# One decoder layer in fp32 on one core: the steps up to the first gate and up products in another order of the table

## The chip, the cores and the metric

The kernel runs on 1 core of one Trainium2 chip. The time is device microseconds (us) of one execution; below, the median of the runs. A core has engines that run side by side, each with its own program that it works through in order: TensorE (PE in the profile, with PEld for its weight loads), VectorE (DVE), ScalarE (ACT), GpSimd (POOL), and SyncE (SP), which here issues nearly all DMAs. An engine waits at an instruction until what it needs has been signalled by the others.

## The reference, cut to what matters

One layer over 512 tokens of width 1024, all in float32: a token mixer between two norms, then a SwiGLU channel mixer between two norms.

```python
h = rms_norm(x, attn_pre_norm)
proj = h @ w_in                       # q, k, v of both head groups, gates
# group A: differential attention, 4 heads, two 64-wide maps each, 128-wide values
p = softmax(mask(q @ k.T * scale)); a = p[0] - lam * p[1]; o = rms_norm(a @ v, diff_subln) * 0.2
# group B: 8 query heads, 2 key/value groups, three branches with sigmoid gates
kc, vc = (silu(blocks(t) @ w1) @ w2 for t in (kc_tok, vc_tok))
o = gate0 * attend(q, kc, vc) + gate1 * attend_selected(q, ks, vs) + gate2 * attend_window(q, kw, vw)
x = x + rms_norm(concat(o_A, o_B) @ w_out, attn_post_norm)
h = rms_norm(x, ffn_pre_norm)
f = (silu(h @ w_gate) * (h @ w_up)) @ w_down
x = x + rms_norm(f, ffn_post_norm)
```

## The kernel before

**Products.** A float32 product is made of three faster ones: each operand is split into a high and a low half (ACT writes the high half, DVE or POOL subtracts it from the operand), and PE multiplies high by high, low by high and high by low into one PSUM tile. So weights come by DMA (`wraw`), are split (`whi`, `wlo`), and are used; activations likewise (`xh`, `xl`; `pth`, `ptl` for attention weights; `oh`, `ol` for head outputs).

**Stages.** The opening loads x and the first weights. Then come the projections (`fm`, `v`, `g` tiles) with the rotary embedding of their results, which go to DRAM (`qk`) and are read back with heads apart (`qst`, `kst`); beside them the compressed keys and values (`cx`, `cst`, `cmp`). Then for each of 12 heads scores (`sc`), maxima, exponentials, scaling, transposes (`tr`), splits of these and the products with the values (`av`); for the compressed branch `scc`, `pc`. The heads' outputs meet the output projection (`mixp`, `mix`), two norms (steps on `u`, `x`, `mixt` with row factors `rr`, transposes `trh`) give the input of the channel mixer, and its first gate and up products (`gu`) follow. These stages overlap. After them come, in loops that the change does not touch, the rest of the gate and up products (`gw`, `block_mul`, L1250) and the down products (`acc`, L1461).

**Order.** The part up to the first gate and up products is written as 32 streams. Each is a Python generator that emits the instructions of one kind of step and yields between steps. A table in the source, `TABLE` (L51), says letter by letter which stream makes its next step; the driver is three lines (L1163 on):

```python
need = {t: next(g) for t, g in streams.items()}
for t in TABLE:
    need[t] = next(streams[t], "end")
```

All instructions of the streams go through a wrapper, `Written` (L222), which keeps them on each engine in the order in which they were emitted. So the table alone fixes, for PE, DVE, ACT, POOL and for SP's queue of DMAs, which instruction stands behind which. (Through the wrapper, all of them have line L230 in the profile; they are told apart by their tiles.) Waits between engines and the rotation of buffers follow from that order: a tile tag has a fixed number of buffers (PSUM: mm 2, tr 2, av 1 and three score tags of 1), and a step that takes a buffer waits for the last reader of the one before it.

The letters that the prediction names, with their function: a `x_loads` L255, b `x_highs` L280, d `constants` L321, S `weights` L419 (a weight's load on SP, its high half on ACT, its low half on DVE), P `projections` L434 (a step is four matmuls of a projection's 24, or some of a compression or value product), R `evictions` L499 (rotary steps on DVE and the store to `qk`), K `compression` L575, Q `loads` L723 (`qst`, `kst`), A `scores` L744, X `maxima` L759, Y `scalings` L788 (on POOL, ACT or DVE by row block), Z `transposes` L814, L `lows` L835 (`ptl`), V `values` L844, O `outputs` L868, J `heads` L894 (the differential heads' norm and the split of all outputs), W `out_weights` L941 (the output projection's weights, and those of the first two gate and up blocks F0 and F1), M `mixes_` L983 (three matmuls each), w, x, y, z `norms` L1129 for the four token blocks, F `gates_` L1140. A step is named by its letter and its number within the letter, from 0: R40 is the 41st R of the table.

Of the kernel before, what the change touches and what calls it, by code (L numbers as in the profile page):

```python
# [48 lines left out]
HEADS = "D2 D3 N4 N5 N6 N7 D0 D1 N0 N1 N2 N3"  # L49
WORDER = "2 3 6 7 0 1 F0 4 5 F1"  # L50
TABLE = (  # L51
    "aaabbcaabbaaPcbPbcbaPaPbaaPbabcPPPPaaccPcPbPbPPPbPPbPcbPPcPdPbdcdPbPPcPbcPSPbcPcPPPPcPPPPcedPPPSSSSeePeP"
    "ePPPPaaPdSeeeRePPeRRSSRRRPRPPPSRPRSRPRSPPPSRRPKPRPPPPRSRPPRPSPSSSaKKPPPPPPPRRSPPPPPSSPSRRRRSSPPPPPRRdRKK"
    "KSRRSKSdPKPKRRRPSPQSdSPSPSSPRSPSPPKSRKKKKKdSRPPSPKKRPdSRdKKPPSRRRSSSdSPPPKdRKKKKKKKPPQSPRRSSKRPSPPPSSPAA"
    "SXPSQEXRRPSRPASPPQRKKPRPPSPSSXXARSARQXPPSEAPXRPKPQKESXGSPRPEESPKSKRPRAdAXPRSSKXdXEKESPRGRRRRPAPPEXGPRRPE"
    "RYRPPPPPRYYYXGPRRPPRGRYPYEYYYPPGSGSPSPPQRPQGGGEZQZQPHPLASAQERXXZAEQHXXARGGSSSSRPEEPERXSYPPGEAXXEGPAPAGYA"
    "HLGXVPRYAELXVREPEXYPSAGEVPVXEOXOYPGXSREPAPERRYRYRPSJJXJYSTPTYZSRRYXTJRPATAPHXZPSLYREJEZPQPAYPRESRJHPSHLX"
    "SRRRRRPJXPAEYYVYPLXZZRPREAPWRXXHRRYJEHVLXPPEEYAZRVHVSRXPWOPQAPOYYPYYWLRSZLHPYWSVLAEYXZXHLZAXWXVPAVRHYXPL"
    "VZYARHYXLEPPPRWVZVHZLPEPTAHESXTRAPVEPEEYVEXWAQVZHYPLWERZPXWPLROHWLWAYEJOWJZWJVPPJYQHXWVYYXLPVXRRAXTVVWYQ"
    "QRWYYVVEEEVTVRZAOHZAEAOJXHLRXLZYEJYHRMZJQARJHEELVMYVVYQRLXVEXYZHYXMRXZAALEEYYQVVHXVZLMAQHLVUZVZYXEJHXYJX"  # L60
    "AHELXALMEZOAAZUHXYHOXXLLYAMYGYVYVZGEVYYYHVGVYGMXLEEUWWEGVXZHZGVGEVLQVHGMOZMQEGHOGMEALLJEJXXAGAVXGEQUEYEY"
    "AQXMGXEGAYVXXEGGWVVMOMEAMGUOWYWGATXAXTJTMYYYYXEMTAJJYEZXJUHZAHWYMMXEALJEWWXLZMYYYYYYYYQXMEZEAJEXHLVWVHZJ"
    "MAXHALEEWVEVLZXWOYYMZOHQAYYXXELHEXAVYVLWXYYYJJEVZEVAAHXJEJEZLVXVHXVZLAJVEEVZMXOAHMXOHLEYLYWJWZZAJXAVHHLE"
    "ELXXYVTTZVYHYYJVXVZAWYLXVAWYWWMMEYHEEZLMHZEHXMLVVTEJYTWLVYOMWZZHYMOLVVJYYYHYZJWVVHLYLVZHMWLVYYZZVVVHHLML"
    "OZOHZLHMVVLZWWWVZHVLHLVVWVVVWOWOMOJOMMJJMMMMJBBBBNBNNNBwwwwwNxNxxwxxwxxxwwwxwwWNwNNNNxWNxwNxxwxwwNxwwxxx"
    "xxwwwNxNxxNxNWWWWNNNyWWyNyNNzyyzFFyyzFyzyFFzzzzyyyFFyzyzyFzyWzzzzyWFyyzzyyFzzzyyyzFzzFz"
)
HP = 400
POOL_LO = "157"
# [1631 lines left out]
```

## Time and profile before

| | |
|---|---|
| median of 3 runs | 654.77 us (654.54, 654.77, 657.61) |
| the profiled execution | 658.55 us |
| its span, first to last instruction | 656.5 us |
| mean granted TensorE clock in it | 0.991 |
| instructions in the span | 11115 |
| busy: PE, DVE, ACT, POOL | 636.7, 545.3, 390.6, 94.4 us |
| chain that ended last, by engine | PE 77%, DVE 12%, DMA 4%, ACT 3% |

The profile is that of one execution, the profiled one, which took some microseconds longer than the median. An engine's busy time counts its instructions from start to end; matmuls are pipelined, so a busy PE is not always one at its peak. In a timeline line the first number is the start in us from the span's start, the second how long the instruction or group took; the bracket at its end gives the idle time before it and what ended that. The chain that ended last is followed back from the last instruction through whatever released each step.

### The profile page before, as it was taken

What the parts mean: (1) busy time and instruction counts of PE and PEld (TensorE: products, weight loads), DVE (VectorE), ACT (ScalarE), POOL (GpSimd) and SP (SyncE); (2) the same over time, 40 slices, a digit from 0 to 9 for tenths busy, and PEclk for the clock granted to TensorE, in tenths of its full rate; (3) what the DMA queues carried; (4) which work ended last, traced back from release to release, by engine and by line L of the source; (5) the groups of instructions that cost most, each with busy time, mean ns of one, the idle gap of its engine ahead of it and who ended that gap; (6) DMA issues with size and microseconds to landing.
All of it is one profiled execution on the core that took longest, in us unless ns stands there. A gap on an engine that the chain in (4) does not pass through costs nothing.

```text
span 656.5 us, 11115 instructions
## 1 busy us (share of the span) xinstructions
PE 636.7 (97%) x4081; PEld 569.9 (87%) x4081; DVE 545.3 (83%) x1050; ACT 390.6 (59%) x821; POOL 94.4 (14%) x100
## 2 busy tenths in 40 slices
PE   9899899999999999999999999999999999999995
PEld 5788789788988888887898999999999998888884
DVE  5757887789789798978999998888888639999866
ACT  7334554575567688955756655655655539675434
POOL 0000001112316236532200000000000101120023
PEclk9799999999999899999999999999999999999999
DMA  8354796715315423145414333223223547984543
GB/s 307 124 162 185 251 309 231 237 36 202 136 35 206 137 106 113 65 178 205 163 34 142 115 103 123 97 97 129 97 97 129 127 131 203 307 257 132 199 90 128
DMA packets 32902, 100.52 MB, mean 153 GB/s; under 512 B 4176, under 2 KB 5072, under 8 KB 31952
## 3 DMA queue, kind: packets, MB, share of 16 engines
q1 hardware_dynamic: 30544, 95.62, 41.8%
q0 software_dynamic: 2304, 4.20, 3.8%
q8 instruction: 32, 0.52, 0.3%
q14 instruction: 22, 0.18, 0.1%
HBM read 85.64 MB, written 12.06 MB: 149 GB/s over the span
## 4 chain that ended last, share of the span: by engine, by line
PE 77%; DVE 12%; DMA 4%; ACT 3%; issue 2%; SPq 0%; DVEq 0%; ACTq 0%
PE gw L1250 28%; PE acc L1461 17%; PE fm L230 9%; PE av L230 4%; PE v L230 4%; PE sc L230 3%; PE mix L230 3%; PE tr L230 3%; PE g L230 2%; DMA wraw<-in_wf 2%; PE scc L230 1%; DVE rr L230 1%; DMA qk<-rope 1%; DVE mixt L230 1%; PE mixp L230 1%
## 5 line engine op out<-in xcount | busy, mean ns | idle before, releaser
L230 POOL TENSOR_TENSOR p<-p,l 128x384 f32<-128x384 f32 (+3 forms) x60 | 54.5, 939 | 126.0 <-DVE l L230 101.3
L230 ACT ACTIVATE p<-p,nm 128x128 f32<-128x128 f32 (+1 forms) x96 | 53.2, 556 | 12.3 <-DVE nm L230 10.3
L230 DVE CUSTOM_DVE_ANT_0 p<-sc,mask_b 128x128 f32<-128x128 f32 (+1 forms) x96 | 44.6, 483 | 7.1 <-PE sc L230 5.5
L230 ACT ACTIVATE whi<-wraw 128x1024 fp32r<-128x1024 f32 (+2 forms) x34 | 34.9, 1034 | 24.3 <-issue 13.1
L230 DVE TENSOR_TENSOR wlo<-wraw,whi 128x1024 fp32r<-128x1024 f32 (+2 forms) x34 | 40.9, 1209 | 8.6 <-ACT whi L230 8.6
L230 ACT ACTIVATE pth<-tr 128x384 fp32r<-128x384 f32 (+1 forms) x60 | 30.7, 521 | 25.1 <-PE tr L230 22.6
L230 DVE TENSOR_TENSOR ptl<-tr,pth 128x384 fp32r<-128x384 f32 (+1 forms) x60 | 35.2, 595 | 10.4 <-ACT pth L230 10.2
L230 PE MATMUL sc<-kst,qst 128*128 128x128 f32 (+1 forms) x192 | 41.3, 331 | 2.2 <-DMA kst<-qk 1.5
L1396 POOL DMA_DIRECT2D dr<-in_wd x8 | 7.0, 880 | 235.8 <-DVE wu L1284 189.3
L230 PE MATMUL fm<-xh,whi 128*128 128x512 f32 x128 | 35.4, 403 | 0.5 <-ACT whi L230 0.5
L230 PE MATMUL fm<-xh,wlo 128*128 128x512 f32 x128 | 35.0, 401 | 0.0
L230 PE MATMUL fm<-xl,whi 128*128 128x512 f32 x128 | 33.7, 394 | 0.0
L230 PEld LDWEIGHTS sc<-kst,qst 128*128 128x128 f32 x192 | 28.8, 189 | 5.3 <-DVE vn L230 1.9
L230 PE MATMUL tr<-ident,p 128*128 128x128 f32 x200 | 31.4, 280 | 1.4 <-DVE ptl L230 1.3
L230 PE MATMUL mix<-ws,oh 128*128 128x512 f32 x84 | 29.6, 403 | 0.0
L230 PEld LDWEIGHTS tr<-ident,p 128*128 128x128 f32 x200 | 24.2, 144 | 5.6 <-DVE ptl L230 1.8
L230 PEld LDWEIGHTS fm<-xl,whi 128*128 128x128 f32 x128 | 24.2, 190 | 5.0
L230 PEld LDWEIGHTS fm<-xh,wlo 128*128 128x128 f32 x128 | 24.1, 192 | 4.9
L230 PEld LDWEIGHTS fm<-xh,whi 128*128 128x128 f32 x128 | 23.5, 192 | 5.0 <-ACT whi L230 1.0
L1461 PE MATMUL acc<-whi,ah 128*128 128x512 f32 x60 | 23.5, 392 | 0.0
L1461 PE MATMUL acc<-whi,al 128*128 128x512 f32 x60 | 23.5, 392 | 0.0
L1461 PE MATMUL acc<-wlo,ah 128*128 128x512 f32 x60 | 23.5, 392 | 0.0
(368 smaller groups left out, 1956.0 us busy)
## 6 DMA issues: line engine op xcount, KB each, us to landing
wraw<-in_wg SPq DMA_DIRECT2D x22, 512.0 KB, 3.3
dr<-in_wd SPq DMA_DIRECT2D x22, 512.0 KB, 4.5
wu<-in_wu SPq DMA_DIRECT2D x19, 512.0 KB, 3.2
wraw<-in_wf SPq DMA_DIRECT2D x16, 512.0 KB, 4.7
qk<-rope SPq DMA_DIRECT2D x7, 1024.0 KB, 4.9
qst<-qk SPq DMA_DIRECT2D x24, 256.0 KB, 2.7
kst<-qk SPq DMA_DIRECT2D x24, 256.0 KB, 4.1
wraw<-in_wo SPq DMA_DIRECT2D x8, 512.0 KB, 3.3
```

Of the source, the lines that this page charges most:

```text
L230: r = getattr(self.eng, name)(*a, **k)
L1250: m = pe.matmul(pt, ww[:, k * P:(k + 1) * P], hx[k], start=(start and n == 0), stop=(n == 11), skip_group_check=True)
L1396: pool.dma_start(t[:, H], wd[pair(p)[0]][:, L], accum_op=OP.add)
L1461: m = pe.matmul(pt, x, y, start=(start and n == 0), stop=(stop and n == 2), skip_group_check=True)
```

## The change

The 1543 letters of `TABLE` are put in another order. Each letter occurs as often as before, so each stream makes the same steps in the same order within itself, and the instructions are the same. Between the streams the order differs: on PE some 1320 of 1787 instructions of this part stand in the same order to one another in both kernels, on DVE 327 of 517, on ACT 237 of 373, on POOL 70 of 76, in SP's queue 107 of 126; none moves by more than about 56 places on PE. The rest of the source, the other tables of order, the buffer counts and the choice of engines are unchanged.

The first and the last three lines of the table in the diff (the eleven between them change in the same manner):

```diff
 TABLE = (
-    "aaabbcaabbaaPcbPbcbaPaPbaaPbabcPPPPaaccPcPbPbPPPbPPbPcbPPcPdPbdcdPbPPcPbcPSPbcPcPPPPcPPPPcedPPPSSSSeePeP"
...
-    "ELXXYVTTZVYHYYJVXVZAWYLXVAWYWWMMEYHEEZLMHZEHXMLVVTEJYTWLVYOMWZZHYMOLVVJYYYHYZJWVVHLYLVZHMWLVYYZZVVVHHLML"
-    "OZOHZLHMVVLZWWWVZHVLHLVVWVVVWOWOMOJOMMJJMMMMJBBBBNBNNNBwwwwwNxNxxwxxwxxxwwwxwwWNwNNNNxWNxwNxxwxwwNxwwxxx"
-    "xxwwwNxNxxNxNWWWWNNNyWWyNyNNzyyzFFyyzFyzyFFzzzzyyyFFyzyzyFzyWzzzzyWFyyzzyyFzzzyyyzFzzFz"
+    "aaaabbbcPcPaPPcaabbPaPaPcbPPPbacPPacPbPPPaPPPPbbPPbcPSPPPbPcbaPPPPPPPPabbcdbbaPSSdabcccbPScccceePPPPSSeP"
...
+    "LYJXAYZYMTEJYXHZELVJXVZVEVVHVVJXAWLEZVVYMYWHEMXHOLETLZYMYYOTHZVYYYYYYVLZHVVVHLJLZHMYZVVLZVWHHVOLYLZMZWJO"
+    "HMHVLLVZZWWWWVHHVLVVLWVVVMOOOOMMMWJJJWJWMBBBBMMBMMNMBWWWwwNwwNNNwNxwwxxxxxxwxNNNwwxwwNxwWxwNxxxxwNwNwwNx"
+    "xxxxNNWNNwWwwxwxxxNNNNNyyyzyWyyzNyyFFzzzyzFFzFFyWFzWyyzFyyFzyyzzzyzyyyzFzzzzzFyFyyzyzzz"
 )
```

More of the change, by code (lines that the diff above doesn't have):

```diff
@@ L51 @@
 TABLE = (
-    "aaabbcaabbaaPcbPbcbaPaPbaaPbabcPPPPaaccPcPbPbPPPbPPbPcbPPcPdPbdcdPbPPcPbcPSPbcPcPPPPcPPPPcedPPPSSSSeePeP"
[L53 to L61, printed above, removed]
@@ L62 @@
-    "AQXMGXEGAYVXXEGGWVVMOMEAMGUOWYWGATXAXTJTMYYYYXEMTAJJYEZXJUHZAHWYMMXEALJEWWXLZMYYYYYYYYQXMEZEAJEXHLVWVHZJ"
-    "MAXHALEEWVEVLZXWOYYMZOHQAYYXXELHEXAVYVLWXYYYJJEVZEVAAHXJEJEZLVXVHXVZLAJVEEVZMXOAHMXOHLEYLYWJWZZAJXAVHHLE"
-    "ELXXYVTTZVYHYYJVXVZAWYLXVAWYWWMMEYHEEZLMHZEHXMLVVTEJYTWLVYOMWZZHYMOLVVJYYYHYZJWVVHLYLVZHMWLVYYZZVVVHHLML"
-    "OZOHZLHMVVLZWWWVZHVLHLVVWVVVWOWOMOJOMMJJMMMMJBBBBNBNNNBwwwwwNxNxxwxxwxxxwwwxwwWNwNNNNxWNxwNxxwxwwNxwwxxx"
-    "xxwwwNxNxxNxNWWWWNNNyWWyNyNNzyyzFFyyzFyzyFFzzzzyyyFFyzyzyFzyWzzzzyWFyyzzyyFzzzyyyzFzzFz"
+    "aaaabbbcPcPaPPcaabbPaPaPcbPPPbacPPacPbPPPaPPPPbbPPbcPSPPPbPcbaPPPPPPPPabbcdbbaPSSdabcccbPScccceePPPPSSeP"
@@ new lines @@
+    "eeePPPPPPeeRSeeRRRaSRPPRPPPPPRRPRRRKPPSSPRdRddSPPPSRRPSPPSPRPPSSPRKPPRPRKPPPKSSSPdPPSSPRRPKRPSSSPRPKKRdR"
+    "RRRRKSPSSKRPPPPSPQRPSSSSPPPPPPdSSKSKKSPRPKPKdKSKRKSKPRKPSSSPPPdRRPSRRSPPPRRRSKKKKSKdKKRSRQPSPKSSKSQdPPSP"
+    "PPPSSSASAXEAXPQRPRKSSPPPKPRdKKPQPXARSRASdPXRXAQRSGSXEXREKPPARXPXPEKSEEASEEKdPASRSRPRPXKPPPPRRYRPGGPYRRRP"
+    "RPRRXPPGEPYYRRRPPPPEPPGYPGGYGRRYSYRSYZGQGQZQPHPSQGPESPXHRRLRPRSPAAAXSPPQXPSPESESRZXGHEXAVSPRXEEGPGYYAXPL"
+    "LXEVSPSAAPXPPYGYARRXYXEXGVVRPAEQOAROYASEJGEPRPXPERYYGPEEXTRXJJYSXRAZSRAHESPEPPSJLTZPEJYXHXSTRRRYPYRXEYAT"
@@ new lines @@
+    "ZPEAJYQLPPRREHJPZLARXVHXLVZPVYSPZRRWRRYHRYXXYAELRPXHEVAZOOYAYREPLPPZHVEVYXVRAAVHYPRLYYZEELPVPYTSQHXJTSPV"
+    "EXXWPWLZZHXRPWWEAPQEPHRXASLVXLVVPYZPYOEXYPAHRLOEZQEAEHAXXYWZPPLPHXZWWPWWWWEERRPLYPYYJWHLVYVVVVRTRARVVXVW"
+    "JRVRTZAJYAERJXRZOHOAJLYXEXYWHEZMQLQHJALRZQJEJZVHQEYYYYXHLXVVXMJMRZYAMHYEXVYLXVEAAZELZWUXYWAVVHYAXVLXEZEV"
+    "MHLXQQAXHEZLEAAOHWJZYXLXEOMZGGVYVVWHLYGUYYYYVHYGYEEWUVVEVXGZLGVEGQVZGXWEHLEMYMZQOOHJYGLGYMGAGXHAVLQVAVQG"
+    "VXGOGMAWMEYXOJYXUAXGMXAEEGYXQGYJTAEXJEEAXXMYAMTXYEETTJJEWAEZAYJXHEZHLYMYYLMYAXZYJWUEXZYAHUHXVWLQVLEZMAVW"
@@ L67 @@
+    "YJXXEZHXVEYEALJHMAXWOOEXWWWLAAYYZYVEYHJVEVJWYMVXMLZWJJEYVYHMWELXZHMELXZHVEVAXELYZXMZVVYAYHHELOXLZATAOEHX"
+    "LYJXAYZYMTEJYXHZELVJXVZVEVVHVVJXAWLEZVVYMYWHEMXHOLETLZYMYYOTHZVYYYYYYVLZHVVVHLJLZHMYZVVLZVWHHVOLYLZMZWJO"
+    "HMHVLLVZZWWWWVHHVLVVLWVVVMOOOOMMMWJJJWJWMBBBBMMBMMNMBWWWwwNwwNNNwNxwwxxxxxxwxNNNwwxwwNxwWxwNxxxxwNwNwwNx"
+    "xxxxNNWNNwWwwxwxxxNNNNNyyyzyWyyzNyyFFzzzyzFFzFFyWFzWyyzFyyFzyyzzzyzyyyzFzzzzzFyFyyzyzzz"
 )
```

## The prediction

> **What bounds the kernel now.** I read the page first: its span, its busy times, the granted clock over the span, and the chain of work that ended last.
>
> ```profile
> span 656.5 us, 11115 instructions
> ...
> PE 636.7 (97%) x4081; PEld 569.9 (87%) x4081; DVE 545.3 (83%) x1050; ACT 390.6 (59%) x821; POOL 94.4 (14%) x100
> ...
> PEclk9799999999999899999999999999999999999999
> ...
> PE 77%; DVE 12%; DMA 4%; ACT 3%; issue 2%; SPq 0%; DVEq 0%; ACTq 0%
> ```
>
> TensorE (PE) is busy for 97% of the span, and the chain runs on it for 77%. The matmuls of both kernels are the same, so an order can only win the time in which PE stands idle between them, plus the time in which its clock is low (the 7 in the second slice and the 8 in the fourteenth). Both are small. The list of waits, for PE, has the largest of its holes by cause (total, times, longest):
>
> ```profile
> PE trh L230 <- DVE mixt L230: 1.7, 4, 0.5
> PE cmp L230 <- DVE rope L230: 1.6, 1, 1.6
> PE sc L230 <- DMA kst<-qk: 1.5, 1, 1.5
> ```
>
> The timeline of PE places them; in brackets stands how long PE was idle before the instruction, and what ended that.
>
> ```profile
> 18.31 0.38 PE L230 MATMUL ssum<-ones,xraw 128*128 128x1 f32 x2 [1.14 <-DVE xraw L230]
> ...
> 80.80 0.35 PE L230 MATMUL cmp<-whi,cst 128*128 128x256 f32 x1 [1.60 <-DVE rope L230]
> ...
> 124.58 0.41 PE L230 MATMUL sc<-kst,qst 128*128 128x128 f32 x2 [1.47 <-DMA kst<-qk]
> ...
> 151.97 0.33 PE L230 MATMUL tr<-ident,p 128*128 128x128 f32 x1 [1.35 <-DVE ptl L230]
> ...
> 204.58 0.49 PE L230 MATMUL mixp<-ws,ol 128*128 128x512 f32 x1 [0.39 <-DVE ol L230]
> ...
> 230.03 0.30 PE L230 MATMUL sc<-kst,qst 128*128 128x128 f32 x1 [0.73 <-DVE ptl L230]
> ...
> 302.13 0.44 PE L230 MATMUL trh<-ident,mixt 128*128 128x128 f32 x2 [0.32 <-DVE mixt L230]
> ...
> 304.40 0.33 PE L230 MATMUL trh<-ident,mixt 128*128 128x128 f32 x1 [0.48 <-DVE mixt L230]
> ...
> 321.56 0.30 PE L230 MATMUL trh<-ident,mixt 128*128 128x128 f32 x1 [0.48 <-DVE mixt L230]
> ...
> 324.21 0.30 PE L230 MATMUL trh<-ident,mixt 128*128 128x128 f32 x1 [0.42 <-DVE mixt L230]
> ```
>
> These ten add up to 8.4 us, 1.3% of the span: that is all there is to win, and each is to be asked of the new order in turn. The chain also says where a gain is carried to the end:
>
> ```profile
> 324.76 5.16 DMA wu<-in_wu
> ...
> 359.08 180.64 PE gw L1250 x1524
> 539.71 110.00 PE acc L1461 x480
> ```
>
> The load at 324.76 takes a slot that the norms' last step frees, VectorE (DVE) works on what it brings, and from 359 PE runs 290 us without a break. Nothing behind the table is touched, so what is saved ahead of 324 comes off the end one for one.
>
> **The change part by part.** I put the steps of both tables side by side on each engine. Each letter occurs as often as before, so nothing is added or removed; only the order on PE, DVE, ACT, POOL and in SP's queue moves. I count the steps of a letter from 0 (R40 is the 41st R).
>
> The opening. At 18.31 PE waits 1.14 us for a DVE step on the raw x. The new order only takes a step of constants from ahead of it on DVE, and puts the three warming matmuls behind the first products. I take -0.1; the ends are -1.1 (the row) and +0.5 (a wait as long as those on mixt).
>
> From 73 to 87. The timelines of DVE and SP and the chain:
>
> ```profile
> 73.31 6.68 DMA qk<-rope
> ...
> 77.81 1.11 DVE L230 TENSOR_TENSOR cst<-cx,cst 128x496 fp32r<-128x496 f32 x1
> 78.82 1.23 DVE L230 TENSOR_TENSOR wlo<-wraw,whi 128x1024 fp32r<-128x1024 f32 x1
> 79.95 1.29 DVE L230 SCALAR_TENSOR_TENSOR rope<-fm,sin 128x512 f32<-128x512 f32 x2
> ...
> 80.00 1.12 SPq L230 DMA_DIRECT2D kst<-qk  x2
> ```
>
> The PSUM buffer for the compression products at 80.80 comes free with the rotary step R40 at 79.95, which stood behind the compression steps K21, K23, K25 (77.81 among them) and the low-half split S43 (78.82). The new order has R40 directly behind R39, so this 1.60 goes. But K27 now stands behind the weight step S46, and its product comes next. Also the store of the rotated q and k (73.31, landing at 80.0) is issued later: DVE has S40 ahead of R35 and R37, one split of 1.23, and SP has the weight loads S41 and S44 ahead of the store and its readback Q1. So the readback at 80.00 goes to about 81.8, and PE has three products moved ahead of the scores A0 and A1 to fill that. I take -0.4 net; the ends are -2.1 (this wait and one of 0.5 behind it both gone) and +1.0 (A0 waits for a load as long as it is late, 1.8, less the few tenths won).
>
> At 124.58 and 151.97. The chain, then the timelines of POOL and DVE:
>
> ```profile
> 119.54 4.90 DMA kst<-qk
> ...
> 129.28 0.93 PE fm L230 x4
> ```
>
> ```profile
> 145.95 6.25 POOL L230 TENSOR_TENSOR p<-p,l 128x256 f32<-128x256 f32 x6 [15.54 <-DVE l L230]
> 146.16 1.21 DVE L230 TENSOR_TENSOR rr<-rr 128x4 f32<-128x4 f32 x2
> ```
>
> Score A12 waits 1.47 for a key load of 4.90. In the new order it stands behind P155 to P159, five steps of four matmuls at 0.93, 4.6 us more of PE work, while the load's place against its own predecessors stays. So I take the whole 1.47 off; the ends are -1.5 and 0. Transpose Z5 waits 1.35 for DVE's L3. It now stands behind P173 to P176 as well (3.7 us). And the scaling Y18, which starts POOL's run at 145.95, is now behind J3 and L3, so that DVE's tiny 4-element steps (1.21 for two at 146.16, beside POOL) have POOL's run behind them. I take the whole 1.35; the ends are -1.35 and 0.
>
> From 204 to 290. V26 to V28 now stand ahead of M1 (204.58), and A48 (230.03) behind M6, M7 and a transpose; against that, A52 will wait some tenths for X66. I take -0.5, between -1.1 and 0. What I price against the change lies behind that. The windows (PE, PEld, DVE, ACT, POOL busy; PEclk; DMA; GB/s) and the chain:
>
> ```profile
> 120.00:140.00 20.00, 18.53 (x96) 15.63 (x95) 18.03 (x53) 12.68 (x36) 2.18 (x3) 1.00 0.46 156
> ...
> 220.00:225.00 5.00, 5.00 (x26) 4.58 (x26) 2.25 (x7) 1.92 (x6) 1.27 (x1) 0.66 0.31 80
> 225.00:230.00 5.00, 4.29 (x27) 3.47 (x27) 3.00 (x5) 3.15 (x8) 0.38 (x1) 1.00 0.74 243
> ...
> 235.00:240.00 5.00, 4.76 (x33) 3.97 (x32) 5.00 (x19) 4.33 (x12) 0.18 (x1) 1.00 0.20 56
> ...
> 265.00:270.00 5.00, 5.00 (x33) 4.26 (x33) 5.00 (x16) 5.00 (x13) 5.00 (x5) 1.00 0.01 3
> ```
>
> ```profile
> 243.32 1.37 PE mix L230 x6
> ```
>
> In the windows at 235 and 265 DVE is as full as PE, and PE is covered by the output projection's matmuls (mix, 0.69 for three). The new order holds back about six of these threes, M16 on, behind the softmax work of the last heads, and moves two low-half splits of the first gate and up weights (W30, W32) from about 268 to about 257 (by the times of their neighbours), ahead of softmax steps: 2 x 1.23 = 2.5 of DVE. In return, DVE gets weight steps and a scaling in the 4.75 us that it has idle between 220 and 230 (2.75 and 2.00 in the two windows). The cost is 0 if that idle time takes all, and 2.5 + 6 x 0.69 = 6.6 if it takes nothing. I take +1.5: half of the two splits (1.2) and a wait of 0.3 as at 302.13, nearer to 0, since PE's own holes between 240 and 290 are tenths now and 4.75 covers 2.5.
>
> From 296 to 324, the norms. The timelines of DVE and POOL:
>
> ```profile
> 298.32 0.75 DVE L230 SCALAR_TENSOR_TENSOR x<-u,rr,x 128x512 f32<-128x512 f32 x1
> ...
> 299.57 1.29 POOL L230 TENSOR_TENSOR ws<-wraw,ws 128x512 fp32r<-128x512 f32 x1 [10.84 <-ACT ws L230]
> ...
> 299.75 1.67 DVE L230 SCALAR_TENSOR_TENSOR x<-u,rr,x 128x512 f32<-128x512 f32 x1
> ...
> 319.57 1.30 POOL L230 TENSOR_TENSOR ws<-wraw,ws 128x512 fp32r<-128x512 f32 x1 [5.20 <-ACT ws L230]
> ...
> 319.61 2.47 DVE L230 SCALAR_TENSOR_TENSOR mixt<-x,rr,gain 128x512 f32<-128x512 f32 x2
> ```
>
> The same DVE step takes 0.75 alone and 1.67 beside a POOL split (W46); the two at 319.61 take 2.47 where two at 0.75 make 1.5 (beside W53). So POOL costs 0.9 and 1.0 on the chain that feeds the four mixt waits. In the new order W46 runs near 291 beside other work, and W53 starts some 4 us earlier, where it meets the step y9; W51 may meet x18. I take half: -0.4 and -0.6; the ends are 0 and -1.9. The Trainium skill ("SBUF — State Buffer", section "SBUF: two separate sides") has VectorE steps with two SBUF inputs and GpSimd steps that read SBUF hold one pair of ports in turn, each for its whole length. The trace agrees: the step of 299.75 ends 0.56 behind POOL's. By that rule each moved split may block another step in full, and this term would be 0 instead of -1.0.
>
> The sum: -0.1 - 0.4 - 1.5 - 1.35 - 0.5 - 0.4 - 0.6 = -4.85, and +1.5, so -3.35. The profiled execution took 658.55 (span 656.5, 2.05 around it), which is 3.8 above the median of 654.77. The terms are waits of fixed length, so I take them off either: a span near 653.2, and a median of 654.77 - 3.35 = 651.4. About what a measurement of this kernel can tell from no change is 0.5%, 3.3 us: faster means under 651.5, slower over 658.0.
>
> **The rivals.** First, given back in place: each hole is only handed on. For it: the store's delay at 73 to 80 and W51 and W53 are seen in the order already, and a table as tightly packed has holes that I cannot see without a trace. Against: A12 and Z5 each have over 3.5 us of new cover. Then 2.85 of these stay, the new waits take 2.0 of them, and it comes to 654.0.
>
> Second, slower: VectorE is the true bound from 120 to 290 (18.03 of 20 at 120, 5.00 of 5 at 235 and 265). Then PE's holes at 124 and 152 are only places where it waits for what DVE gives anyway, their 2.85 come back as waits later on, and the full 6.6 of splits and held-back products shows: -4.85 + 2.85 + 6.6 = +4.6, so 659.4. It decides if under 1 us of the 4.75 idle on DVE at 220 to 230 is filled. Against: that idle time itself, and a wait at 124.58 that is for a DMA and not for DVE.
>
> Third, the clock. PE counts as busy all through 220 to 225, and its clock was 0.66 there: 0.34 x 5 = 1.7 us lost, amid steps of many 32-column matmuls that the new order packs still closer. If the dip goes, -1.7 more: 649.7; if a second comes, near 117, where two such steps now follow each other, +1.7: 653.1. The Trainium skill ("TensorE: Matmul & The Clock Gate", sections "What's actually happening" and "HAM oscillation — how this bites in real kernels") has the clock fall to half after an idle window of about 3.4 us. The size of the dip agrees (1.7 is half of 3.4), the cause does not: no row shows PE idle so long, and the hole of 1.47 at 124.58 brought none (clock 1.00 at 120 to 140). By that rule the change would leave the clock alone.
>
> Fourth, everything goes and nothing new comes: the ten waits together with what stands behind them, about -8: 646.8.
>
> **How the numbers follow.** My forecast 0.48 (its own range 649 to 653.5: over half of it, 0.30, under 651.5); given back 0.24 (same); VectorE as the bound 0.18 (slower); the clock 0.03 (faster); everything 0.07 (faster). That the table does not do what it says is left out, since the program's order is the table's. So faster 0.30 + 0.03 + 0.07 = 0.40, slower 0.18, same 0.42. The range reaches from 646.5 (everything gone) to 658.5, which holds the mild half of the second rival's way up and leaves out some 0.15 above and 0.05 below.
>
> **What would show it.** Right: no wait over 0.5 at the products cmp<-rope, sc<-kst and tr<-ptl of these places; the DVE steps at about 296 and 316 at 0.75; DVE over 3.5 of 5 in the windows that now have 2.25 and 3.00. Wrong: PE waits of 1 us and more on DVE between 235 and 290, or the chain on DVE there (second rival); as many holes as before under other names, 7 to 9 us in all (first); a clock under 1.00 near 117 (third). The forecast is wrong if the start of the gate products now at 359.08 does not move ahead by 2 to 5 us.

## The result, and the profile after

The changed kernel takes 652.12 us (median of 8 runs, 649.61 to 652.97), the kernel before 655.03 (8 runs, 654.54 to 657.61): a ratio of 0.9938, with an interval of 0.9919 to 0.9957. That is faster by 0.4 to 0.8%, 2.9 us by the medians and 4.1 by the ratio; the forecast was 651.4, 3.35 less. The median lies 0.6 above the 651.5 under which the prediction called the kernel faster; the interval lies wholly below 1.

The page of the changed kernel, in the lines that were shown of the one before:

```profile
span 649.7 us, 11129 instructions
...
PE 631.3 (97%) x4081; PEld 567.0 (87%) x4081; DVE 542.2 (83%) x1050; ACT 390.8 (60%) x821; POOL 90.2 (14%) x100
...
PEclk9899999999999999999999999999999999999998
...
PE 82%; DVE 7%; DMA 4%; ACT 4%; issue 2%; SPq 1%; DVEq 0%; ACTq 0%
```

The span of the profiled execution is 6.8 us shorter, more than the medians say. The clock has a part in that: it was 0.991 in the profiled execution before and 0.995 in this one. Before, it was 0.67 from 20 to 30 us and 0.66 from 220 to 225, together 5.0 us of clock lost; after, only 0.83 from 20 to 30, 1.7 us. That is 3.3 of the 6.8. The chain has 7% on DVE in place of 12%: it now stays on PE from 319 on, where before it ran over DVE from 324 to 359. PE itself was idle for only 0.5 us in that stretch before.

```profile
319.55 1.89 PE gu L230 x16
321.44 22.57 PE gu L1233 x144
344.01 188.86 PE gw L1250 x1596
532.87 110.01 PE acc L1461 x480
```

The waits of PE in the changed kernel (total, times, longest):

```profile
PE sc L230 <- DMA kst<-qk: 1.8, 4, 0.8
PE fm L230 <- ACT xh L230: 1.5, 1, 1.5
PE trh L230 <- DVE mixt L230: 1.5, 1, 1.5
...
PE tr L230 <- DVE ptl L230: 1.1, 1, 1.1
PE cmp L230 <- DVE cst L230: 0.8, 1, 0.8
...
PE trh L230 <- DVE rr L230: 0.4, 1, 0.4
```

and the places of the larger ones in its timeline:

```profile
81.76 0.38 PE L230 MATMUL cmp<-whi,cst 128*128 128x256 f32 x1 [0.82 <-DVE cst L230]
...
84.74 0.30 PE L230 MATMUL sc<-kst,qst 128*128 128x128 f32 x1 [0.75 <-DMA kst<-qk]
...
222.82 0.30 PE L230 MATMUL sc<-kst,qst 128*128 128x128 f32 x1 [0.63 <-DMA kst<-qk]
...
253.03 0.33 PE L230 MATMUL tr<-ident,p 128*128 128x128 f32 x1 [1.06 <-DVE ptl L230]
...
318.26 0.30 PE L230 MATMUL trh<-ident,mixt 128*128 128x128 f32 x1 [1.48 <-DVE mixt L230]
```

The holes of 1.47 and 1.35 at 124.58 and 151.97 have no successor: PE's windows show no gap between 120 and 130 or between 148 and 158.

```profile
120.00:130.00 10.00, 10.00 (x52) 8.49 (x51) 8.85 (x27) 6.74 (x17) 0.38 (x2) 1.00 0.83 287
148.00:158.00 10.00, 10.00 (x78) 9.54 (x77) 9.05 (x18) 7.03 (x18) 5.05 (x5) 1.00 0.37 134
```

The hole of 1.60 at 80.80 has become one of 0.82 and one of 0.75. New are the waits at 222 (a key load), 253 and 318, and that of an opening product on `xh` (1.5).

### The profile page after: what moved, and what is told of

It reads as the page before. It is cut to its first block, busy times and chain, and to the rows that moved or that the text cites. A ratio compares the mean times of both kernels' runs of the same rounds, so it can differ in the third digit from the quotient of the medians.

```text
span 649.7 us, 11129 instructions
## 1 busy us (share of the span) xinstructions
PE 631.3 (97%) x4081; PEld 567.0 (87%) x4081; DVE 542.2 (83%) x1050; ACT 390.8 (60%) x821; POOL 90.2 (14%) x100
## 4 chain that ended last, share of the span: by engine, by line
PE 82%; DVE 7%; DMA 4%; ACT 4%; issue 2%; SPq 1%; DVEq 0%; ACTq 0%
PE gw L1250 29%; PE acc L1461 17%; PE fm L230 11%; PE av L230 4%; PE sc L230 4%; PE gu L1233 3%; PE v L230 3%; PE mix L230 3%; PE tr L230 2%; DMA kst<-qk 2%; PE g L230 2%; DMA wraw<-in_wf 1%; DVE rr L230 1%; DVE wlo L230 1%; DMA qk<-rope 1%
## 5 line engine op out<-in xcount | busy, mean ns | idle before, releaser
L230 POOL TENSOR_TENSOR p<-p,l 128x384 f32<-128x384 f32 (+3 forms) x60 | 49.9, 863 | 143.0 <-DVE l L230 94.8
```

The costliest lines, as they stand in the source:

```text
L230: r = getattr(self.eng, name)(*a, **k)
```

## The experiments

My theory was that of the sum: holes at 124 and 152 that go for good, about 1 us of new waits and shifts elsewhere. The rivals were VectorE as the bound (each hole comes back between 200 and 290) and the clock. All ratios are to the kernel before, in runs on the same chip.

**The first 100 us alone.** The changed table up to letter 380, then the letters that are left, in the order before.

```diff
-TABLE = BEFORE
+TABLE = AFTER[:380] + (the rest of the letters, as in BEFORE)
```

> The table of the changed kernel for its first 380 letters (to about 99 us), then the remaining letters in the order of the kernel before. If the time follows the listed holes of TensorE: only the hole at 80.80 changes (1.60 goes, two waits of about 0.8 and 0.7 stay), so 654.0 to 654.7 against 655.0, and the holes at 124 and 152 are still there with 1.4 each. If VectorE is the bound from 120 on: 655.0, no change. If the clock is what differs: the dips in the profile move, the median stays.

Measured: 657.3, ratio 1.0018 (1.0005 to 1.0030). Slower, which neither theory said. The profile shows why it is no fair test of that part: where the two tables meet, a score of the compressed branch waits for a query load.

```profile
104.57 0.25 PE L230 MATMUL scc<-kch,qst 128*128 128x32 f32 x1 [1.27 <-DMA qst<-qk]
```

That seam (1.27) is in neither kernel. These twelve runs also have a lower mean clock than the kernel before beside them, 0.9922 against 0.9937, which is worth up to 1.0 us (0.0015 of 655). So what the first 100 us alone are worth stays open. The holes at 124 and 152 were still there (1.24 and 1.35), as expected, though the first now ends with a DVE step (`vn`) and not with the key load.

**The first 200 us alone.**

```diff
-TABLE = BEFORE
+TABLE = AFTER[:880] + (the rest of the letters, as in BEFORE)
```

> The table of the changed kernel for its first 880 letters (to about 199 us), then the remaining letters in the order before. If the time follows the holes: those at 80, 124 and 152 are gone, 1.0 + 1.5 + 1.35 less 0.5 of small new ones, so about 651.7. If VectorE is the bound: the 2.85 of 124 and 152 come back as waits on VectorE between 200 and 290, so about 654.5. If the clock alone differs: 655.0.

Measured: 651.49, ratio 0.9929 (0.9909 to 0.9948). All of the gain of the whole change (0.9938) is there with only its first 200 us; from 200 on the new order brings nothing on balance. In the forecast, too, the terms from 200 on add up to 0 (-0.5 + 1.5 - 1.0). The holes did not come back as waits on VectorE: PE's list has one of 0.6 on `l` there, and else the waits of the norms.

**One step: Y18 behind J3 and L3, in the kernel before.**

```diff
-R82 Y18 X26 T2 J3 R83 P170 ... S79 L3 Y19
+R82 X26 T2 J3 R83 P170 ... S79 L3 Y18 Y19
```

> The kernel before with one step moved: Y18, which releases the run of six row scalings on GpSimd, stands behind J3 and L3 on VectorE. If it was GpSimd's run that stretched J3's four tiny steps (2.78 us), J3 takes about 0.75, L3 ends some 2 us earlier, and the hole of 1.35 at 152 goes: 653.7 against 655.0. If TensorE only waits there for what VectorE gives anyway: the hole moves, 655.0. If J3 is slow for another reason: it still takes over 2 us and the hole stays.

Measured: 654.16, ratio 0.9972 (0.9959 to 0.9986), 1.8 us less. In the kernel before, the last two of J3's four steps, behind the two of 1.21 at 146.16, were these:

```profile
147.40 0.97 DVE L230 TENSOR_SCALAR rr<-rr 128x4 f32<-128x4 f32 x1
148.41 0.53 DVE L230 TENSOR_TENSOR rs<-rr 128x4 f32<-128x4 f32 x1
```

DVE and POOL in this run:

```profile
144.86 0.36 DVE L230 TENSOR_TENSOR rr<-rr 128x4 f32<-128x4 f32 x2
145.25 0.17 DVE L230 TENSOR_SCALAR rr<-rr 128x4 f32<-128x4 f32 x1
145.45 0.16 DVE L230 TENSOR_TENSOR rs<-rr 128x4 f32<-128x4 f32 x1
...
147.88 0.69 DVE L230 TENSOR_TENSOR ptl<-tr,pth 128x512 fp32r<-128x512 f32 x1
```

```profile
149.03 5.73 POOL L230 TENSOR_TENSOR p<-p,l 128x256 f32<-128x256 f32 x6 [19.50 <-DVE l L230]
```

J3's four steps take 0.75 us from first to last, where they took 2.78 beside POOL's run, and PE's list has no wait on `ptl` any more. The gain, 0.9 to 2.7 by its interval, holds the 1.35 of the hole.

**One step: A12 and X16 behind P158, in the kernel before.**

```diff
-X15 A12 R71 G10 ... P155 ... R73 X16 S73 Y9 P157 P158 G12
+X15 R71 G10 ... P155 ... R73 S73 Y9 P157 P158 A12 X16 G12
```

> The kernel before with one score moved: A12 and its maxima X16 stand behind P155 to P158, 3.7 us of projection matmuls, so that they cover the key load. If the hole of 1.47 at 124.58 is only that load's lateness: it goes, 1.4 us less than before, 0.998. If VectorE bounds the stretch (second rival): the hole moves behind X16, no change, 1.000.

Measured: 654.98, ratio 0.9982 (0.9967 to 0.9998), 1.2 us less. The wait on `kst` has left PE's list; the largest that remain are those that the step doesn't touch:

```profile
PE cmp L230 <- DVE rope L230: 1.6, 1, 1.6
PE trh L230 <- DVE mixt L230: 1.4, 3, 0.5
...
PE tr L230 <- DVE ptl L230: 1.3, 1, 1.3
```

The mean clock of these runs was 0.9939, that of the kernel before beside them 0.9926; up to 0.9 of the 1.2 us can be clock, so that here the vanished hole is better evidence than the time. In the run of Y18 the clock was no higher than before (0.9932 and 0.9937).

By the ratios the two edits bring 1.2 + 1.8 = 3.0 of the 4.1 us, each give or take about 1; no run has both together. VectorE as the bound falls with these two and with the first 200 us.

**J31 behind L41, in the changed kernel.** The wait at 253 was the largest new one ahead of the norms. In the changed kernel DVE and POOL show this ahead of it:

```profile
248.11 1.47 DVE L230 TENSOR_TENSOR rr<-rr 128x4 f32<-128x4 f32 x2
249.62 0.76 DVE L230 TENSOR_SCALAR rr<-rr 128x4 f32<-128x4 f32 x1
250.41 0.96 DVE L230 TENSOR_TENSOR rs<-rr 128x4 f32<-128x4 f32 x1
251.29 1.21 DVE L230 TENSOR_TENSOR wlo<-wraw,whi 128x1024 fp32r<-128x1024 f32 x1
252.42 0.55 DVE L230 TENSOR_TENSOR ptl<-tr,pth 128x384 fp32r<-128x384 f32 x1
```

```profile
245.62 5.73 POOL L230 TENSOR_TENSOR p<-p,l 128x256 f32<-128x256 f32 x6 [0.41 <-DVE l L230]
```

```diff
-L39 Z40 W31 J30 J31 E83 ... W32 E84 L40 ... L41 X86
+L39 Z40 W31 J30 E83 ... W32 E84 L40 ... L41 J31 X86
```

> The changed kernel with one step moved: J31, four tiny VectorE steps that took 3.26 us at 248.11 beside GpSimd's run, stands behind L41 and so behind that run. If J31 beside GpSimd is what made L40 and so transpose Z42 late: J31 takes about 0.75, the wait of 1.1 at 253 goes, 1.0 to 1.2 us less than the changed kernel, about 651.0. If it is the weight split W32 that I priced (ahead of L40 in both): L40 is still late by its 1.2, the wait stays at 0.5 or more, and the time is 651.6 to 652.1.

Measured: 650.09, ratio 0.9912 (0.9890 to 0.9934) where the changed kernel has 0.9938. PE's wait on `ptl` is gone from its list, though the split W32 still stands ahead of L40. J31 starts at 253.68 there, as POOL's run ends, and takes 0.74. So it was J31 beside POOL that made the wait, and not the split. That the time follows is not settled: the two intervals overlap, and in this run's profile the wait for the key load at 224 has grown to 1.16 from 0.63.

**The opening in the order before, the rest changed.**

```diff
-TABLE = AFTER
+TABLE = BEFORE[:91] + (the rest of the letters, as in AFTER)
```

> The changed kernel with the first 91 letters in the order before (up to the sums of squares at 18.3), the rest as in the changed kernel. If the new opening costs time (it was 0.6 to 0.9 us later at the sums of squares in the profiles): 0.6 less than the changed kernel, 651.5. If that is only when the first loads land, which differs from run to run: 652.1, with a wait of about 1 at the warming matmuls instead of at P1.

Measured: 651.2, ratio 0.9925 (0.9901 to 0.9949). The sums of squares begin at 18.36 and the wait on `xh` is gone, but the interval holds the changed kernel's 0.9938: not settled. Of the profiles with the new opening, five list a wait on `xh` (1.5, 1.4, 0.9, 0.8, 0.9) and three list none, though their first steps are the same. It hangs on when the first loads land: in the five, ACT starts its second split of x between 7.9 and 8.5 us, in the three between 6.7 and 6.9. The six profiles with the old opening have it between 6.9 and 7.4, so that a part of the new opening in this is not ruled out.

**K26 and K27 ahead of S46, in the changed kernel.**

```diff
-P108 S46 P109 K26 S47 S48 K27 S49
+P108 K26 K27 S46 P109 S47 S48 S49
```

> The changed kernel with K26 and K27 ahead of S46 and P109, so that the product P112 doesn't wait for K27 behind a split of 1.2 us. If each wait of TensorE counts by itself: the 0.8 at 81.8 goes, 651.3 against 652.1. If the key load Q1 is the bound there, late because the store of q and k is: the wait only moves to A0 at 84.7, which grows from 0.8 to 1.6, and the time stays at 652.1.

Measured: 651.89, ratio 0.9928 (0.9902 to 0.9953), against 652.12 no difference. PE's timeline has the waits where they would go:

```profile
81.22 0.39 PE L230 MATMUL cmp<-wlo,cst 128*128 128x256 f32 x1 [0.70 <-DVE wlo L230]
...
84.42 0.30 PE L230 MATMUL sc<-kst,qst 128*128 128x128 f32 x1 [0.98 <-DMA kst<-qk]
```

The 0.82 on K27 became 0.70 on the split S46 behind it, and the wait for the key load 0.98.

**The norms.** In the changed kernel DVE, POOL and ACT show between 308 and 319:

```profile
308.22 2.45 DVE L230 SCALAR_TENSOR_TENSOR x<-u,rr,x 128x512 f32<-128x512 f32 x2
...
314.98 0.59 DVE L230 TENSOR_SCALAR rr<-rr 128x1 f32<-128x1 f32 x2
316.78 0.42 DVE L1224 TENSOR_TENSOR ff<-ff,gu 128x256 f32<-128x256 f32 x1 [1.22 <-ACT ff L1223]
317.12 0.21 DVE L230 TENSOR_SCALAR rr<-rr 128x1 f32<-128x1 f32 x1
317.37 1.42 DVE L230 SCALAR_TENSOR_TENSOR mixt<-x,rr,gain 128x512 f32<-128x512 f32 x2
```

```profile
308.24 1.87 POOL L230 TENSOR_TENSOR ws<-wraw,ws 128x512 fp32r<-128x512 f32 x1 [0.86 <-ACT ws L230]
```

```profile
315.07 1.28 ACT L1223 ACT_TABLE_LOAD   x1
316.37 0.66 ACT L1223 ACTIVATE ff<-gu 128x256 f32<-128x256 f32 x2
```

Two things hold the chain of the norms: W53 on POOL beside y9, and a product `ff` from behind the table, which stands in DVE's queue ahead of the last of z15's three steps and waits there 1.22 us for ACT, which loads its table of functions. Both were mended together and one at a time.

```diff
-        dve.tensor_tensor(sl, sl, pts[1][:, s0:s1], OP.mult)
+        with tc.issue_after(row_of["d"]):
+            dve.tensor_tensor(sl, sl, pts[1][:, s0:s1], OP.mult)
...
-W50 w19 w20 ... x22 x23 ... y3 W51 y4 ... y9 W52 F6 z7 W53
+W50 W51 w19 w20 ... x22 x23 W52 W53 ... y3 y4 ... y9 F6 z7
```

> The changed kernel with two further edits in the norms: W51 to W53 moved ahead on ScalarE and GpSimd, so that GpSimd's split W53 runs beside VectorE steps that read PSUM (about 300) and not beside y9; and the product ff<-ff,gu, which waits on VectorE's queue for a ScalarE table load (1.2 us) ahead of z15's last step, held behind the last htl step. If the two waits of TensorE on mixt at 314 and 318 (0.8 and 1.6) come from these: y9 and y11 take 1.5 in place of 2.45, the waits shrink to under 1.0 together, and the time is 650.3 to 651.2 against 652.1. If the gate and up matmuls after 320 wait for VectorE anyway: 652.1.

Measured: 650.14, ratio 0.9904 (0.9882 to 0.9925). No wait on `mixt` is left at 314 or 318. Further on, PE has new waits of 0.7 and 0.4 behind 346, on ACT.

Only the product `ff` held back:

> Half of the norms' edits on the changed kernel: only the ff product held behind the last htl step. If the table load behind which VectorE stood is what made z16 late: the wait at 318 goes from 1.6 to 0.4 or less, and the time is 1.2 less, 651.0 (0.992). If y9's stretch by W53 sets z16 as well: the wait stays above 1, and 651.8.

Measured: 651.23, ratio 0.9925 (0.9906 to 0.9944). z15 and z16 run through:

```profile
315.02 0.84 DVE L230 TENSOR_SCALAR rr<-rr 128x1 f32<-128x1 f32 x3
315.89 1.41 DVE L230 SCALAR_TENSOR_TENSOR mixt<-x,rr,gain 128x512 f32<-128x512 f32 x2
```

and the wait of 1.48 is gone, while 0.4 stays at 314; but waits of 0.6 and 0.5 come at 347 and 352, where gate products need what ACT and DVE make of the first ones.

Only the splits moved ahead:

> The other half: only W51 to W53 moved ahead. y9 and y11 in 1.5 us in place of 2.45; the waits on mixt at 314 go (0.8), while the table load still holds z15, so the wait at 318 stays at 1 or more. By the holes 0.8 less than the changed kernel, 651.3 (0.993); if the table load takes it up, 652.1.

Measured: 651.95, ratio 0.9934 (0.9909 to 0.9958). The two x steps take 1.41 now, and the product `ff` still waits 1.22 us for ACT; PE's wait stands at 316 now and is 1.31 in place of 1.48, and the 0.4 at 314 is gone:

```profile
307.42 1.41 DVE L230 SCALAR_TENSOR_TENSOR x<-u,rr,x 128x512 f32<-128x512 f32 x2
...
314.95 0.42 DVE L1224 TENSOR_TENSOR ff<-ff,gu 128x256 f32<-128x256 f32 x1 [1.22 <-ACT ff L1223]
```

The two edits one at a time are each within the changed kernel's interval; together they lie below its median by 2 us, at the edge of what their intervals tell apart. The traces say more. From the end of the last `mix` product to the end of the last `trh`, the same matmuls take 13.98 us in the changed kernel, 12.94 with only the splits moved, 12.46 with only `ff` held back and 11.43 with both. From the first `gw` product to the first `acc` they take 188.86, 188.84, 190.57 and 190.54. So holding `ff` back wins 1.5 us and hands 1.7 on, while the moved splits win 1.0 and keep it; the runs of the splits alone do not confirm this (651.95).

**All findings together, on the changed kernel**: the old opening, J31, W51 to W53 and `ff`, by the diffs above.

> The changed kernel with the three findings together: the opening in the order before, J31 behind L41, W51 to W53 ahead and the ff product behind the last htl step. If each wait of TensorE ahead of 324 comes off the end by itself: 0.5 + 1.1 + 2 less than the changed kernel, 0.9865 to 0.989 of the kernel before (about 648). If what is won ahead of 320 is given back where the gate products wait for VectorE's and ScalarE's sums (two waits of 0.9 and 0.6 stood at 347 to 352 in the run with the norms' edits): about 650, 0.990 to 0.9915.

Measured: 650.72, ratio 0.9911 (0.9883 to 0.9938), runs from 646.68 to 652.18. That is better than the kernel before but not better than two of its parts alone. The number is that of the second forecast, but not for its reason: of the two waits on ACT's `cy` only one, of 0.5, is in its list, and there is 1.87 at A0.

```profile
85.24 0.30 PE L230 MATMUL sc<-kst,qst 128*128 128x128 f32 x1 [1.87 <-DMA kst<-qk]
```

Its windows there (PE, PEld, DVE, ACT, POOL busy; clock) show a dip of the clock right behind that:

```profile
80.00:85.00 5.00, 2.54 (x19) 2.13 (x17) 3.45 (x5) 1.70 (x2) 0.00 (x0) 1.00 0.55 193
85.00:90.00 5.00, 4.76 (x17) 4.03 (x18) 3.05 (x8) 2.15 (x5) 0.00 (x0) 0.66 0.98 337
```

Its clock was 0.992 or 0.993 in five of six runs, where most others have 0.993 to 0.996; the run of 646.68 had 0.997. That the dip comes in all five was not seen, since only one has a profile. The dip costs 1.7 us (0.34 of 5). What the wins add up to stays open.

**The kernel before, a second time.** No edit.

> The kernel before, unchanged, for a second profile of it. If the clock's dip to 0.66 at 220 to 225 belongs to that order (its many 32-column matmuls): it is there again, 1.7 us. If it came by chance: the clock is 1.00 there, PE's holes at 80, 124, 152 and in the norms are as before, and the span is about 653.

Measured: 656.12, ratio 1.0013 (0.9991 to 1.0035), span 652.8 with a clock of 0.996. The window in question:

```profile
220.00:225.00 5.00, 5.00 (x38) 4.59 (x37) 1.98 (x5) 2.44 (x7) 1.28 (x1) 1.00 0.47 139
```

The dip at 220 is not there, with the same order: the order alone does not bring it. Against this profile the changed kernel's span is 3.1 us shorter, at nearly the same clock (0.995), and that agrees with the medians. The down products, which nothing ahead of them can hide a gain from, start 3.1 us earlier too (532.87):

```profile
535.95 110.01 PE acc L1461 x480
```

## Why the prediction was right, step by step

The time came out close to the forecast, but in part by luck. The second profile of the kernel before and that of the changed kernel have nearly the same clock, and some places in them can be compared one by one:

| place on PE | before | changed | won since the place above |
|---|---|---|---|
| first `cht` starts | 65.88 | 66.59 | -0.71 |
| last `mix` ends | 309.13 | 305.58 | 4.26 |
| last `trh` ends | 322.07 | 319.56 | -1.04 |
| first `gw` starts | 346.37 | 343.85 | 0.01 |
| first `acc` starts | 535.78 | 532.71 | 0.55 |

The column adds up to 3.07 us. The forecast had 0.1 won up to `cht`, 2.25 in the second row (-0.4 - 1.5 - 1.35 - 0.5 + 1.5), 1.0 in the norms, and nothing behind them. So the second row won 2.0 more than forecast and the norms lost 1.0 in place of winning it, and these two errors cancel. Of the 4.3, PE's idle time makes 3.0 (6.9 before, 3.8 after). The other 1.2 is PE's busy time for the same 1432 matmuls, 236.4 before and 235.1 after at a clock of 1.00: a sum of holes has no term for that, and no run shows its cause. Single profiles leave about 1 us of play in the second row: seven profiles with the changed order there, or with one step of it moved, and without a dip of the clock took between 238.0 and 240.1 us for it. Nor were the ten holes of 8.4 us all there was to win, as the prediction has it: PE was idle for 19.8 us of the span before (656.5 less 636.7), 3.0 of them in the first 30 us.

- **124 and 152** (-1.5 and -1.35): right in cause, and the two holes are gone in full: PE is idle for 3.3 us between 100 and 200 in the second profile before, and for 0.2 after. Moved alone in the kernel before, they bring 1.2 and 1.8 us, and J3 falls from 2.78 to 0.75 once POOL's run is behind it.
- **80 to 87** (-0.4): right as argued. R40's 1.60 went, and K27 behind S46 (0.82) and the late readback (0.75) took nearly all of it; what remains as won is the wait of 0.5 at 87, which the forecast had at one end of its range and which has gone. Mending K27 only handed the wait on.
- **The opening** (-0.1): not confirmed. In the changed kernel's profile P1 waits 1.5 for `xh`; before, the warming matmuls stood at that place. In three other profiles with this opening there was no such wait, and the 0.9 us by which the run with the old opening was faster is inside the noise.
- **204 to 240** (-0.5): the holes at M1 and at `ptl` went, but A39, A45, A48 wait for key loads now. The prediction named a wait of A52 on X66 and did not follow the loads.
- **The stretch to 290** (+1.5): the one large wait that came is 1.06 at 253, and its cause was not the one named. The prediction priced two splits of 2.5 in a full queue and the held-back products; it was again four tiny steps in POOL's run, J31, 3.26 us. What the new order cures at 146 it brings back at 248. This term and the one before it make +1.0 together; the changed kernel needs 0.3 us more for the second row of the table than the run of the first 200 us alone (238.65), so together they came out near 0.
- **The norms** (-1.0): the step that failed. W46 did leave x11, and PE's list has no wait of the first two blocks any more (0.8 before), and W53 left the two `mixt` steps that took 2.47 at 319.61: they take 0.75 and 0.74 now. But that 1.0 us reaches nobody. The product `ff`, which is not in the table, stands in DVE's queue between z15's steps in both kernels, and needs ACT's table load. Before, DVE came to it late enough to find it ready:

```profile
321.02 1.28 ACT L1223 ACT_TABLE_LOAD   x1
```

```profile
322.74 0.42 DVE L1224 TENSOR_TENSOR ff<-ff,gu 128x256 f32<-128x256 f32 x1
```

Now DVE comes earlier and waits the 1.22 us, and the wait of 1.48 at 318 follows. From the end of the last x step to `ff` it is 3.12 us before (319.62 to 322.74) and 3.11 after (313.67 to 316.78). And W53 met y9 as feared: 2.45 for two steps that take 1.41 without it, 1.0 lost. The prediction priced W53 by the DVE steps beside it alone and had no term for the table load to which they lead. The term was -1.0, with 0 as the other value named; it came out as +1.0, by the table's third row, which is y9's loss. PE's waits before `trh` are 1.9 in place of 1.7 in all, but those of the kernel before stand in part ahead of the last `mix`. Behind the norms 0.55 was won between the first `gw` and the first `acc`. So the step that what is saved ahead of 324 comes off the end one for one does not hold quite either: here 0.55 more came off, and with `ff` held back 1.7 less than in the changed kernel.
- **The sign that was to show it.** The gate products were to move ahead by 2 to 5 us. Their part of the chain begins elsewhere now, but between the two profiles of like clock the first of them moved by 2.5 and the down products behind them by 3.1. One sign of the second rival came too, a PE wait of 1 us on DVE between 235 and 290; it was the only one, that of J31.
- **The rivals.** VectorE as the bound: no, shown by the single steps. Given back: true of the norms and of 80 to 87, not of the two large holes. The clock: its dip in the first profile does not belong to the order. But the clock has not dropped out: its mean over the eight runs of the changed kernel is 0.9944, over the 58 runs of the kernel before beside the experiments 0.9932. If all of that shows in the time, it is 0.8 us of the difference; whether the new order has a part in it is not shown.

## What to carry to other kernels

Where PE is busy for nearly all of the span, ask of each hole which single step made it late: three letters of 1543 (Y18; A12 and X16), moved in two runs, brought 1.8 and 1.2 us where the whole reordering brought 4.1. A queue that runs in program order turns any operation that waits in it into a wait for all behind it, also one that the reordered part doesn't list; look for what lies between. A wait that is mended counts only if the next one behind it is earlier.

## What the runs showed of the hardware

A VectorE step of 4 elements per partition, 0.16 to 0.17 us alone, took up to 0.97 beside GpSimd's multiplications of SBUF tiles, so that four of them cost 3.26 us instead of 0.75. One of GpSimd's multiplications there takes about 1.0 (5.73 and 6.25 for six). It fits what the Trainium skill ("SBUF — State Buffer", section "SBUF: two separate sides") says of the shared port pair: the loser waits for the other's whole instruction. A step on 512 elements went from 0.75 to 1.2 (2.45 for two), a step on 4 from 0.17 to 0.97.

Every profile has the clock low between 20 and 30 us, behind the sums of squares: 0.83 over these 10 us in twelve of the fourteen, 0.67 and 0.70 in the other two. Two further dips were seen between 30 and 640 us, both 0.66 over 5 us, or 1.7 us: in the kernel before at 220, where PE showed no gap, and in the last combination at 85, behind a window in which PE was busy for 2.54 of 5. The run of the norms' edits had 2.63 of 5 in the same window, and no dip behind it:

```profile
80.00:85.00 5.00, 2.63 (x20) 2.24 (x19) 3.55 (x5) 1.64 (x2) 0.00 (x0) 1.00 0.52 163
```

What decides is not shown. The mean clock of the runs lay between 0.987 and 0.998, and 0.001 of 650 us is 0.65 us, so a difference of 2 us between two kernels needs several runs of each.
